# LayerNorm of x + residual on one core: another order and another cut of the 27 DMA transfers

## The chip, the core and the metric

The kernel runs on one core of a Trainium2 chip. The core has a tensor engine (PE), a vector engine (VectorE, DVE in the profile), a scalar engine (ScalarE, ACT), GpSimd (POOL) and a sync engine (SyncE, SP) that here only issues DMA transfers. Sixteen DMA engines move data between HBM (the large outer memory) and SBUF (the on-chip memory of 128 partitions). The metric is the device time of one execution in microseconds.

## The reference

```python
def setup_inputs():
    batch, seq, dim = 16, 1024, 512
    ...

def reference(x, residual, gamma, beta, eps):
    z = x + residual
    mean = np.mean(z, axis=-1, keepdims=True)
    var = np.var(z, axis=-1, keepdims=True)
    z_norm = (z - mean) / np.sqrt(var + eps)
    return (gamma * z_norm + beta).astype(np.float32)
```

x, residual and the output have 16 x 1024 = 16,384 vectors of 512 numbers in float32, 33.55 MB each. Each vector is normalised by itself.

## The kernel before

**Rows.** The 16,384 vectors are spread over 128 partitions, 128 to each. The kernel counts in "rows": row j is the j-th vector of every partition, 128 x 512 numbers or 256 KB, and there are 128 rows. They form two blocks of 64; within a block, the 64 vectors of a partition lie one behind the other in HBM (line 76), so a transfer of n rows reads or writes one run of n x 2 KB for each partition.

**Buffers.** SBUF holds `zbuf` with 64 rows, into which x is loaded and from which the output is stored, and `rbuf` with 32 rows, into which the residual is loaded. Row j uses place j mod 64 of the one and j mod 32 of the other. Both are rings: a load of a later row may start only when the row that had its place is done with it.

**Compute.** Work goes in turns of 4 rows, 32 turns in all, the same for every plan. For each turn, in order:
- POOL adds x and residual into `rbuf` (line 178), after the loads that hold these rows have landed.
- ACT takes the negative mean of each row (line 201), the sum of squares around it (line 211) and the standard deviation of the 4 rows (line 220).
- DVE computes (z + negative mean) x gamma into `zbuf` (line 239), the reciprocal `rstd` (line 247), and then times `rstd` plus beta (line 253). The semaphore `rstd` says that the turn's rows of `rbuf` are free, the semaphore `out` that its output is ready.

PE is used only at the start, to spread gamma and beta over the partitions (line 131).

**Transfers.** All loads and stores are issued by SP, in the order of the string PLAN (line 19). A word is a kind (x, r for residual, o for output), the first row and the number of rows: `x4+12` loads rows 4 to 15 of x. Each transfer has its own semaphore. Before it issues a transfer, SP waits for what that transfer needs, and all later transfers wait behind it (lines 145 to 160):

```python
if kind == "x":
    while gone < len(stores) and stores[gone][0] < lo + n - Z_ROWS:
        nc.sync.wait_ge(so[gone], 16)
        ...
elif kind == "r":
    if lo + n > R_ROWS:
        last = (lo + n - R_ROWS) // TURN - 1
        nc.sync.wait_ge(s_rstd[last % Z_TURNS], last // Z_TURNS + 1)
    ...
else:
    if lo + n > seen:
        nc.sync.wait_ge(s_out, lo + n)
```

So an x load waits until the stores that read its places of `zbuf` have landed; a residual load waits until DVE is done with the rows 32 earlier; a store waits for the output of its last row. After the last issue, SP waits for all stores (lines 163 to 167). The plan of before has 27 transfers: 10 of x, 10 of the residual and 7 of the output. The first two are issued ahead of the others, at the start of the program (lines 269 to 277).

Of the kernel before, what the change touches and what calls it, by code (L numbers as in the profile page):

```python
# [15 lines left out]
R_ROWS = 32  # L16


PLAN = """
x0+4 r0+4 x4+12 r4+16 x16+12 r20+12 x28+12 x40+16 x56+8  # L20
r32+16 o0+24 r48+16 x64+24 r64+16 o24+24 r80+16 x88+16
r96+12 o48+16 x104+8 r108+8 x112+16 r116+12
o64+24 o88+16 o104+16 o120+8
"""


ADDS = [4] * 32
# [11 lines left out]
def kernel(  # L39
# [22 lines left out]
    moves = []  # L62
    for word in PLAN.split():
        kind, (lo, n) = word[0], map(int, word[1:].split("+"))
# [248 lines left out]
```

## Time and profile before

| what | value |
|---|---|
| median of 5 runs | 237.93 us (237.88 to 238.36) |
| the profiled execution | 237.91 us |
| its span, from the first to the last instruction | 236.6 us |
| data moved | 100.67 MB: 67.11 MB read, 33.55 MB written |
| mean rate over the span | 426 GB/s |
| first store issued | at 63.55 us, after x loads up to row 63 and residual loads up to row 47 |
| last load landed | near 197.8 us |
| last store issued | at 225.4 us |

Times within the profile are microseconds from the start of the span. "Busy" is the time in which an engine executes instructions; for the DMA it is the share of time in which its 16 engines move packets. In a table of instructions, a row gives the start, the busy time, the engine, the line, the operation with its output and inputs, how many are merged in the row, and in brackets how long the engine had been idle before and what released it. In a table of waits, a row gives who waited for whom, the time in total, the number of waits and the longest. In a table of windows, the columns are the window, its length, the busy time and count of each engine, the tensor engine's clock, the DMA share and GB/s; packets are counted whole, so a short window can show more than 1. Issuing a DMA takes SP about 0.33 us and is not the transfer itself.

### The profile page before, as it was taken

The page shows a single profiled execution, that of the slowest core. Times are in us where ns is not written, and L with a number is a line of the kernel's source. Part 1 is how long each engine was busy: PE and PEld are TensorE (multiplying, and loading weights), DVE is VectorE, ACT ScalarE, POOL GpSimd, SP SyncE. Part 2 cuts the span into 40 slices and gives each one's busy share as a digit, 9 for nine tenths or more (in the row PEclk, how much of TensorE's full clock was granted, in tenths as well). Part 3 has the DMA queues.
Part 4 walks back from the last instruction along what each step waited for, and adds up shares of the span by engine and source line. Part 5 has one row for each costly group of instructions (what it writes and reads, how often), then busy time and mean ns, then how long its engine had stood idle before and what let it go on. Part 6 is the DMA issues. An engine that isn't in the chain of part 4 may idle for free.

```text
span 236.6 us, 988 instructions
## 1 busy us (share of the span) xinstructions
PE 3.7 (2%) x4; PEld 1.2 (0%) x4; DVE 177.3 (75%) x290; ACT 184.0 (78%) x545; POOL 144.1 (61%) x36
## 2 busy tenths in 40 slices
PE   0600000000000000000000000000000000000000
PEld 0100000000000000000000000000000000000000
DVE  0009009999996299979997999899999999879900
ACT  2090099999972999799979998899999999799100
POOL 0600899994009990999179926899939275970000
DMA  8999999999999999999999999999999999999997
GB/s 301 454 454 392 461 407 457 443 443 391 429 465 399 440 446 471 416 399 416 427 474 457 393 432 421 421 427 432 413 435 460 414 432 461 416 421 443 432 410 316
DMA packets 3892, 100.67 MB, mean 426 GB/s; under 512 B 434, under 2 KB 434, under 8 KB 436
## 3 DMA queue, kind: packets, MB, share of 16 engines
q1 hardware_dynamic: 3888, 100.67, 99.3%
q10 hardware_dynamic: 4, 0.00, 0.0%
HBM read 67.11 MB, written 33.55 MB: 426 GB/s over the span
## 4 chain that ended last, share of the span: by engine, by line
ACT 44%; DMA 37%; POOL 8%; DVE 6%; issue 1%; SPq 0%; DVEq 0%; POOLq 0%
DMA rbuf<-in_residual_dram 37%; ACT junk_s L211 22%; ACT junk_m L201 19%; POOL rbuf L178 8%; DVE zbuf L239 5%; ACT std L220 2%; DVE zbuf L253 1%; DVE rstd L247 0%; SPq L140 0%; DVEq L231 0%; POOLq L175 0%
## 5 line engine op out<-in xcount | busy, mean ns | idle before, releaser
L178 POOL TENSOR_TENSOR rbuf<-zbuf,rbuf 128x2048 f32<-128x2048 f32 x32 | 143.9, 4522 | 67.0 <-DMA rbuf<-in_residual_dram 57.1
L239 DVE SCALAR_TENSOR_TENSOR zbuf<-rbuf,nm,gamma_p 128x512 f32<-128x512 f32 x128 | 87.1, 743 | 44.9 <-ACT std L220 44.9
L201 ACT ACTIVATE junk_m<-rbuf 128x512 f32<-128x512 f32 x128 | 74.3, 580 | 30.9 <-POOL rbuf L178 30.8
L211 ACT ACTIVATE junk_s<-rbuf,nm 128x512 f32<-128x512 f32 x128 | 88.8, 694 | 1.0
L253 DVE SCALAR_TENSOR_TENSOR zbuf<-zbuf,rstd,beta_p 128x512 f32<-128x512 f32 x128 | 87.1, 744 | 1.1
L211 ACT ACTIVATION_READ_ACCUMULATOR junk_s<-rbuf,nm 128x1 f32 x128 | 23.9, 187 | 0.0
L201 ACT ACTIVATION_READ_ACCUMULATOR junk_m<-rbuf 128x1 f32 x128 | 23.9, 187 | 0.0
L220 ACT ACTIVATE std<-ssq,eps_t 128x4 f32<-128x4 f32 x32 | 9.5, 297 | 1.0
L247 DVE RECIPROCAL rstd<-std 128x4 f32<-128x4 f32 x32 | 5.5, 171 | 0.0
L192 ACT ACT_TABLE_LOAD x1 | 1.3, 1283 | 2.7 <-PEq L60 2.7
L131 PE MATMUL gamma_p<-gb_row,ones 1*128 1x512 f32 x2 | 2.0, 1120 | 6.8 <-DMA gb_row<-in_gamma_dram 6.8
L131 PE MATMUL beta_p<-gb_row,ones 1*128 1x512 f32 x2 | 1.9, 1056 | 0.0
L126 DVE MEMSET ones<- 1x128 f32 x1 | 0.2, 165 | 2.0 <-PEq L60 2.0
L131 PEld LDWEIGHTS beta_p<-gb_row,ones 1*128 1x128 f32 x2 | 0.7, 332 | 1.0 <-DMA gb_row<-in_beta_dram 0.5
L131 PEld LDWEIGHTS gamma_p<-gb_row,ones 1*128 1x128 f32 x2 | 0.5, 304 | 6.8 <-issue 6.8
L294 POOL MEMSET const-float32-0.0<- 128x1 f32 x1 | 0.1, 99 | 0.2 <-issue 0.2
L294 POOL MEMSET const-bfloat16-1.0<- 128x1 bf16 x1 | 0.1, 102 | 0.0
L294 POOL MEMSET const-uint8-127<- 128x1 uint8 x1 | 0.1, 102 | 0.0
L294 POOL MEMSET const-float32-1.0<- 128x1 f32 x1 | 0.1, 99 | 0.0
L127 DVE MEMSET eps_t<- 128x1 f32 x1 | 0.1, 59 | 0.0
## 6 DMA issues: line engine op xcount, KB each, us to landing
rbuf<-in_residual_dram SPq DMA_DIRECT2D x5, 4096.0 KB, 21.5
out_dram<-zbuf SPq DMA_DIRECT2D x3, 6144.0 KB, 30.1
zbuf<-in_x_dram SPq DMA_DIRECT2D x3, 4096.0 KB, 19.3
out_dram<-zbuf SPq DMA_DIRECT2D x3, 4096.0 KB, 26.1
zbuf<-in_x_dram SPq DMA_DIRECT2D x3, 3072.0 KB, 28.9
rbuf<-in_residual_dram SPq DMA_DIRECT2D x3, 3072.0 KB, 23.4
zbuf<-in_x_dram SPq DMA_DIRECT2D x1, 6144.0 KB, 23.9
zbuf<-in_x_dram SPq DMA_DIRECT2D x2, 2048.0 KB, 43.2
```

The costliest lines, as they stand in the source:

```text
L126: nc.vector.memset(ones[:, :], 1.0).then_inc(s_const, 1)
L127: nc.vector.memset(eps_t[:, :], float(eps)).then_inc(s_const, 1)
L131: nc.tensor.matmul(dest[:, :], ones[:, :], gb_row[:, k * D : (k + 1) * D], start=True, stop=True).then_inc(s_pe, 1)
L178: nc.gpsimd.tensor_tensor(out=z, in0=part(zbuf, Z_ROWS, lo, n), in1=z, op=ALU.add).then_inc(s_sum[lo // TURN % R_TURNS], 1)
L192: act.preload_act_table_set("sqrt_and_others")
L201: i = act.activation(out=junk_m[k][:, :], in_=part(rbuf, R_ROWS, r, 1), func=ACT.Identity, scale=-inv_d, accum_out=column(nm, r),)
L211: i = act.activation(out=junk_s[k][:, :], in_=part(rbuf, R_ROWS, r, 1), func=ACT.Square, bias=column(nm, r), accum_out=column(ssq, r),)
L220: act.activation(out=column(std, rows[0], TURN), in_=column(ssq, rows[0], TURN), func=ACT.Sqrt, bias=eps_t[:, 0:1], scale=inv_d,).then_inc ...
L239: dve.scalar_tensor_tensor(out=part(zbuf, Z_ROWS, r, 1), in0=part(rbuf, R_ROWS, r, 1), scalar=column(nm, r), in1=gamma_p[:, :], op0=ALU.ad ...
L247: dve.reciprocal(out=column(rstd, rows[0], TURN), in_=column(std, rows[0], TURN)).then_inc(s_rstd[j], 1)
L253: i = dve.scalar_tensor_tensor(out=z, in0=z, scalar=column(rstd, r), in1=beta_p[:, :], op0=ALU.mult, op1=ALU.add,)
L294: nc = _bacc.Bacc("TRN2", target_bir_lowering=False, num_devices=1)
```

## The change

Only the string PLAN changes. The compute instructions and their order stay as they are; the order, the sizes and with them the waits of SP's transfers change.

```diff
-PLAN = """
-x0+4 r0+4 x4+12 r4+16 x16+12 r20+12 x28+12 x40+16 x56+8
-r32+16 o0+24 r48+16 x64+24 r64+16 o24+24 r80+16 x88+16
-r96+12 o48+16 x104+8 r108+8 x112+16 r116+12
-o64+24 o88+16 o104+16 o120+8
-"""
+PLAN = """x0+4 r0+4 x4+12 r4+16 r20+12 x16+12 r32+4 x28+12 o0+8 x40+24 r36+16 o8+16 r52+12 x64+24 r64+16 o24+24 r80+16 x88+4 r96+8 x92+20 o48+16 r104+12 x112+16 r116+12 o64+24 o88+24 o112+12 o124+4"""
```

- The first four transfers stay. r20 and x16 trade places.
- Four rows of the residual (r32+4) are loaded ahead of x28, and the first store, now of 8 rows, follows x28. Before it stood behind the loads of x40, x56 and r32+16 too.
- x40+16 and x56+8 become one transfer of 24 rows; r32+16 and r48+16 become r32+4, r36+16 and r52+12; the first 24 rows of output are stored as 8 and 16 in place of 24.
- x88+16 and x104+8 become x88+4 and x92+20; r96+12 and r108+8 become r96+8 and r104+12.
- The last 64 rows are stored as 24, 24, 12 and 4 in place of 24, 16, 16 and 8.

There are now 28 transfers: 9 of x, 11 of the residual and 8 of the output. All lines below the plan move up by 5.

## The prediction

> **What bounds the kernel now.** I read the page's first table, then its DMA line, then the Sync queue's waits, then the start times of GpSimd's adds, which date the landings. The busiest engines leave much of the span free, and the 16 DMA engines leave almost none:
>
> ```profile
> PE 3.7 (2%) x4; PEld 1.2 (0%) x4; DVE 177.3 (75%) x290; ACT 184.0 (78%) x545; POOL 144.1 (61%) x36
> ...
> DMA  8999999999999999999999999999999999999997
> ...
> q1 hardware_dynamic: 3888, 100.67, 99.3%
> ```
>
> ScalarE (ACT) is busy 184.0 of 236.6 us. The one DMA queue that carries the data is busy 99.3% of all 16 engines' span, and the only slices below 9 tenths are the first and the last. The chain of waits names ACT for 44% and a residual load for 37%, but that chain follows single releases; the transfers behind it queue without a hole. The queue's own waits say the same from the issuing side:
>
> ```profile
> SPq L140 <- DVE rstd L247: 113.3, 7, 44.0
> SPq L140 <- DVE zbuf L253: 65.7, 5, 24.6
> SPq L140 <- DMA out_dram<-zbuf: 34.7, 3, 13.3
> ```
>
> SyncE (SP) waits 213.7 us (113.3 + 65.7 + 34.7), yet the DMA engines stay busy: each wait is spent while earlier transfers still run. So the time is: start, plus the sum of all transfers one after another, plus the last landing. An order changes it only if it leaves the DMA engines without work, or changes the cost of the transfers themselves.
>
> **The price of a transfer.** An add starts about 0.06 us after the load that it waited for, so these rows date landings:
>
> ```profile
> 24.57 31.39 POOL L178 TENSOR_TENSOR rbuf<-zbuf,rbuf 128x2048 f32<-128x2048 f32 x7 [12.38 <-DMA rbuf<-in_residual_dram]
> 70.88 17.94 POOL L178 TENSOR_TENSOR rbuf<-zbuf,rbuf 128x2048 f32<-128x2048 f32 x4 [14.92 <-DMA rbuf<-in_residual_dram]
> 95.17 17.99 POOL L178 TENSOR_TENSOR rbuf<-zbuf,rbuf 128x2048 f32<-128x2048 f32 x4 [6.35 <-DMA rbuf<-in_residual_dram]
> 119.60 17.98 POOL L178 TENSOR_TENSOR rbuf<-zbuf,rbuf 128x2048 f32<-128x2048 f32 x4 [6.44 <-DMA rbuf<-in_residual_dram]
> 143.88 9.01 POOL L178 TENSOR_TENSOR rbuf<-zbuf,rbuf 128x2048 f32<-128x2048 f32 x2 [6.29 <-DMA rbuf<-in_residual_dram]
> 153.59 17.99 POOL L178 TENSOR_TENSOR rbuf<-zbuf,rbuf 128x2048 f32<-128x2048 f32 x4 [0.70 <-DMA zbuf<-in_x_dram]
> 175.62 4.53 POOL L178 TENSOR_TENSOR rbuf<-zbuf,rbuf 128x2048 f32<-128x2048 f32 x1 [4.03 <-DMA zbuf<-in_x_dram]
> 180.52 4.53 POOL L178 TENSOR_TENSOR rbuf<-zbuf,rbuf 128x2048 f32<-128x2048 f32 x1 [0.37 <-DMA rbuf<-in_residual_dram]
> 190.23 4.53 POOL L178 TENSOR_TENSOR rbuf<-zbuf,rbuf 128x2048 f32<-128x2048 f32 x1 [5.17 <-DMA zbuf<-in_x_dram]
> 197.82 4.53 POOL L178 TENSOR_TENSOR rbuf<-zbuf,rbuf 128x2048 f32<-128x2048 f32 x1 [3.05 <-DMA rbuf<-in_residual_dram]
> ```
>
> Two pairs of neighbours hold one load each: x88+16 takes 153.59 - 143.88 = 9.71 us and r108+8 takes 180.52 - 175.62 = 4.90 us. So a row of the plan costs (9.71 - 4.90) / 8 = 0.601 us and a transfer 4.90 - 8 x 0.601 = 0.09 us beside its rows. The other gaps, less this price, show what a **turn from loads to stores** costs. 24.57 to 70.88 holds 76 rows in 6 transfers (46.22 by the price, +0.09), and the next 24.29 us o0+24 and r48+16 (24.22, +0.07): 0.16 for the first turn. 95.17 to 119.60 (40 rows, 24.43, +0.21) and the stretch to 143.88 (24.28, +0.06): 0.27 for the second. 153.59 to 175.62 holds r96+12, o48+16 and x104+8 (21.91, measured 22.03): 0.12. r116+12, ahead of the last stores, took 7.59 where 7.30 was due: 0.29. From 197.82 to the last landing near 236.5 come 64 rows in four stores (38.82 by the price, 38.7 measured), so 0.1 of that comes back. A turn costs 0.12 to 0.29, 0.2 in the middle; turns from stores to loads show nothing of their own.
>
> **The change, part by part.**
> *Bytes.* Both plans move 128 rows of x, residual and out: nothing.
> *One transfer more* (28 for 27): +0.09 us. The upper end is the other small transfer shown: r0+4 was issued at 0.44 and landed 7.1 later, at 7.54; x0+4 landed at 4.9; 2.64 for 4 rows is 0.24 over 4 x 0.601, with the start of the kernel in it.
> *One turn more.* Before, stores follow loads four times (o0, o24, o48, o64); after, five times (o0+8, o8+16, o24, o48, o64): +0.12 to +0.29, I take 0.18.
> *One more issue on SP* (0.33 us) and one more wait at its end lie beside running transfers; without that cover they would cost 0.35.
> *Swap of x16 and r20:* the rows that need either (16 to 27) need both; the adds of rows 4 to 15 run on meanwhile. Nothing.
> *The last store of 4 rows* in place of 8 shortens nothing: it waits in the queue, not for compute. Before, the last store was issued at 225.4 and landed 11.2 us later, of which its own 8 rows are 4.9, so 6.3 us of other stores ran ahead of it.
>
> **Where a wait could empty the queue.** The cover of a wait is the work still queued when the waiting instruction issues. A first byte takes about 1.0 us from the issue (the first issue is at 0.00, no DMA is busy before 1.00). Compute goes by its rows: an add 4.5 us, ACT 5.77 a turn of 4 rows, DVE 2.85 to rstd and 2.75 more to the output.
> - o0+8 waits for the output of row 7. ACT ends that turn near 35.0, DVE near 40.5; r32+4 and x28+12 hold the queue until 24.4 + 40 rows in 4 transfers = 48.8. Cover 8.3.
> - x64+24 waits for o8+16 to land, with only r52+12 queued: 7.3, where the shortest such cover before was 9.7 (x88+16 behind r80+16). x112+16 behind r104+12 is alike: 7.3.
> - r64+16 waits for rstd of row 47: r36+16 lands near 78.1 (24.4, 88 rows, 7 transfers, a turn), the add ends at 82.7, ACT ends rows 36 to 47 at 100.0, rstd 102.8. The queue runs until r36's 78.1 + 17.2 (o8+16, r52+12, a turn) + 14.5 (x64+24) = 109.8. Cover 7.0.
> - r96+8 (rstd of row 71, near 137.5) has r80 and x88+4 ahead of it until 146.4: 8.9. Behind it stand x92+20 and o48+16, which need nothing later.
> - o112+12 waits for row 123: the last load lands near 198.0, outputs of rows 120 to 123 are ready near 219.8, and o64+24 and o88+24 run to 227.1: 7.3. o124+4, ready near 225.5, has 8.9.
> All exceed the 1.0 by 6 us or more, so no hole is due, and nothing of the moved waits reaches the end.
>
> **Sum.** +0.09 + 0.18 = +0.27 us on the profiled execution (237.91 us, a span of 236.6 and 1.3 around it); the median of the runs is 237.93. Forecast **238.2 us**, +0.1%.
>
> **A rule that speaks against it.** Measured, a transfer of 4 rows (1024 KB) takes 2.64 us in the queue at most, and an extra transfer 0.09 to 0.24. The Trainium skill, "DMA: Bandwidth & Descriptors", section "Anatomy of one DMA", gives each DMA a fixed cost of about 2.0 us, on the GpSimd path; were that serial here, the 28th transfer alone would make 239.9. The rows above contradict that for queued transfers: landings follow at 0.601 us a row with 0.09 between.
>
> **Rivals.**
> 1. *Nothing at all* (0.2): turn and transfer vanish in the engines' own spread: 237.9. For it: the last turn gave back 0.1 of 0.29.
> 2. *The turns cost more* (0.15). Two turns now stand where all engines run in step; in the trace's packet records the turn from r32+16 to o0+24 has the largest single delay, 0.60 us on one 32 KB packet. With 0.24 for the transfer and 0.4 for the turn: 238.55, slower.
> 3. *The queue runs dry* at x64+24 (0.04), and x112+16 alike, since 12 rows are all that is behind the store waited for. It decides once landing, wait and first byte take over 7.3 us. Each us beyond costs a us at each of the two: 1 us short gives 240.2. Against it: 1.0 us measured, and the same shape with 9.7 left no hole.
> 4. *The engines end together* (0.06). At the end a few engines run alone:
>
> ```profile
> 234.50:235.00 0.50, 0.00 (x0) 0.00 (x0) 0.00 (x0) 0.00 (x0) 0.00 (x0) 1.00 0.84 360
> 235.00:235.50 0.50, 0.00 (x0) 0.00 (x0) 0.00 (x0) 0.00 (x0) 0.00 (x0) 1.00 0.16 66
> 235.50:236.00 0.50, 0.00 (x0) 0.00 (x0) 0.00 (x0) 0.00 (x0) 0.00 (x0) 1.00 0.08 33
> ```
>
> The DMA share (second column from the end) falls to 0.16 and 0.08: after 235.00 that adds up to 0.12 us of all engines ((0.16 + 0.08) x 0.5), and the last landing comes 1.5 us later. If the new order evened out two thirds of it (an estimate), 1.0 us would go: 237.2. Against it: each engine still gets the same bytes, and one turn more adds spread.
>
> **How the numbers follow.** Forecast 0.55 (238.0 to 238.4), rival 1 0.2, rival 2 0.15, rival 3 0.04, rival 4 0.06. The range 237.7 to 238.65 holds the forecast, rivals 1 and 2, and leaves out about a tenth and the outer parts of these. A measurement of this kernel tells about 0.2% (0.48 us) from no change: faster is rival 4 (0.06), slower rivals 2 and 3 (0.19), within 0.2% the rest (0.75).
>
> **What would show it.** Right: the queue again at 99% of its span, no slice but the first and last below 9; the add released by r36+16 near 78, that by r52+12 near 95, the last one near 198.1; o124+4 issued near 225.5 and landing near 236.8. Wrong: a slice in the middle below 9, an add late by a microsecond or more against these times, the last store landing soon after its issue, or a row price other than 0.60.

## The result

The changed kernel takes 238.68 us (median of 21 runs, 237.93 to 240.12), the kernel before 237.92 us (41 runs, 237.63 to 238.63): a ratio of 1.0036, 95% interval 1.0025 to 1.0046, or +0.86 us by the ratio. It is slower, by three times the 0.27 us that were forecast.

The profiled execution took 238.31 us with a span of 237.0, 0.4 us more than before. The page still shows a kernel that waits for its transfers:

```profile
PE 3.7 (2%) x4; PEld 1.2 (0%) x4; DVE 177.2 (75%) x290; ACT 183.9 (78%) x545; POOL 144.0 (61%) x36
...
DMA  8999999999999999999999999999999999999997
...
q1 hardware_dynamic: 4032, 100.67, 99.3%
```

The engines' busy times are within 0.1 us of before, the DMA engines are at 99.3% again, and no slice in the middle falls below 9. So no wait emptied the queue. The rows of the adds date the landings (start and busy time in us, engine, line, operation, how many; in brackets the idle time before and what ended it):

```profile
24.44 13.43 POOL L173 TENSOR_TENSOR rbuf<-zbuf,rbuf 128x2048 f32<-128x2048 f32 x3 [12.35 <-DMA rbuf<-in_residual_dram]
38.98 22.47 POOL L173 TENSOR_TENSOR rbuf<-zbuf,rbuf 128x2048 f32<-128x2048 f32 x5 [1.10 <-DMA zbuf<-in_x_dram]
78.56 31.40 POOL L173 TENSOR_TENSOR rbuf<-zbuf,rbuf 128x2048 f32<-128x2048 f32 x7 [17.11 <-DMA rbuf<-in_residual_dram]
119.97 17.98 POOL L173 TENSOR_TENSOR rbuf<-zbuf,rbuf 128x2048 f32<-128x2048 f32 x4 [10.02 <-DMA rbuf<-in_residual_dram]
144.20 13.50 POOL L173 TENSOR_TENSOR rbuf<-zbuf,rbuf 128x2048 f32<-128x2048 f32 x3 [6.24 <-DMA rbuf<-in_residual_dram]
163.71 13.50 POOL L173 TENSOR_TENSOR rbuf<-zbuf,rbuf 128x2048 f32<-128x2048 f32 x3 [6.01 <-DMA zbuf<-in_x_dram]
...
197.82 13.51 POOL L173 TENSOR_TENSOR rbuf<-zbuf,rbuf 128x2048 f32<-128x2048 f32 x3 [2.78 <-DMA rbuf<-in_residual_dram]
```

With the prediction's price (0.601 us a row, 0.09 a transfer) the stretches between these rows show where time is lost. From 24.44 to 78.56 come 88 rows in 7 transfers, 53.52 by the price and 54.12 measured: 0.60 lost. This stretch holds the turn from x28+12 to o0+8 and ends with r36+16, the load ahead of the next turn, so the rows alone don't say at which of the two. The trace also has a record of when each of the 16 engines landed its share of a transfer. By the last share, x28+12 took 0.57 longer than its price and r36+16 0.01: the first turn cost it. From 78.56 to 119.97 (o8+16 to the landing of r64+16) come 68 rows in 4 transfers: 41.23 due, 41.41 measured, 0.18 lost. The next two stretches, with the turns at o24+24 and at o48+16 (the latter seen from 163.71 on), cost 0.01 and about 0.1.

One sum is the same for both plans. Between the landings of r4+16 and r64+16 lie 156 rows in either plan, in 10 transfers before and 11 after. This stretch took 119.60 - 24.57 = 95.03 us before and 119.97 - 24.44 = 95.53 after: +0.50, of which 0.09 is the transfer. The rest of the kernel is as long as before: from the add of r64+16 to the last landing it is 236.5 - 119.60 = 116.9 us before and 236.9 - 119.97 = 116.9 after. (The span grows by 0.4 and not by 0.5, since r4+16 landed 0.13 earlier in this execution.)

### The profile page after: what moved, and what is told of

Its sections match the earlier page's. It is cut to its first block, busy times and chain, and to the rows that moved or that the text cites. A ratio compares the mean times of both kernels' runs of the same rounds, so it can differ in the third digit from the quotient of the medians.

```text
span 237.0 us, 990 instructions
## 1 busy us (share of the span) xinstructions
PE 3.7 (2%) x4; PEld 1.2 (0%) x4; DVE 177.2 (75%) x290; ACT 183.9 (78%) x545; POOL 144.0 (61%) x36
## 3 DMA queue, kind: packets, MB, share of 16 engines
q1 hardware_dynamic: 4032, 100.67, 99.3%
## 4 chain that ended last, share of the span: by engine, by line
ACT 43%; DMA 36%; POOL 8%; DVE 6%; issue 1%; SPq 0%; ACTq 0%; DVEq 0%; POOLq 0%
DMA rbuf<-in_residual_dram 26%; ACT junk_s L206 22%; ACT junk_m L196 19%; DMA zbuf<-in_x_dram 10%; POOL rbuf L173 8%; DVE zbuf L234 5%; ACT std L215 2%; DVE zbuf L248 1%; SPq L135 0%; DVE rstd L242 0%; ACTq L189 0%; DVEq L226 0%; ACTq L194 0%; POOLq L170 0%; ACTq L190 0%
```

## The experiments

Theory E: the early extra turn from loads to stores costs the time. Its rivals, as they came up: N, every turn costs alike; S, a short store behind a load makes the turn dear; C, a thin queue ahead of a wait costs time even where it doesn't run empty; D, another order of the loads costs it; Q, the name of C at first; and that the middle or the end of the new plan costs it. In the expectations of the first four runs E is called A, N is called B, and the last rival is called C; in the later ones C is the thin queue. All times are against the kernel before on the same chip, with the 95% interval of the ratio.

### Which half of the plan

`after_again` is the changed kernel once more.

> The changed plan once more, as the yardstick for the runs beside it. Theory A (the first turn from loads to stores, x28 to o0+8, is dear and varies from run to run): +0.3 to +1.0 us against the kernel before, single times spread over 2 us, and in the profile x28+12 landing 0.5 us or more later than its 12 rows cost. Theory B (every turn and every transfer costs a little, 0.1 to 0.3 us): +0.2 to +0.4 with a spread like that of before.

Measured: 1.0021 (1.0005 to 1.0037), median 238.21 beside 237.89, single times 237.86 to 239.83.

`start_only` has the changed plan up to r80+16 and the plan of before behind it:

```diff
-... r80+16 x88+4 r96+8 x92+20 o48+16 r104+12 x112+16 r116+12 o64+24 o88+24 o112+12 o124+4
+... r80+16 x88+16 r96+12 o48+16 x104+8 r108+8 x112+16 r116+12 o64+24 o88+16 o104+16 o120+8
```

> The changed plan up to r80+16, the plan of before from x88+16 on: 28 transfers, 5 turns. Theory A: as slow as the whole change, +0.3 to +1.0, with the same spread of single times. Theory B: +0.2 to +0.4, tight. Theory C (the new end, stores of 24, 24, 12 and 4 rows, and the new middle cost the time): within 0.1 us of before.

Measured: 1.0029 (1.0015 to 1.0043), single times 238.03 to 239.82. `rest_only` is the other half: the plan of before up to r80+16, the changed one behind it.

> The plan of before up to r80+16, the changed plan from x88+4 on: 27 transfers, 4 turns. Theories A and B: within 0.15 us of before. Theory C: +0.4 or more, since the whole cost sits in this half.

Measured: 0.9995 (0.9986 to 1.0003), single times 237.61 to 238.19. The whole cost, with the spread of single times, sits in the first part of the plan. The new middle and the new end, the last store of 4 rows included, cost nothing that can be measured, and gain nothing.

### Is it turns as such, or something at this one

`late_turn` adds a turn to the plan of before at another place:

```diff
-... r64+16 o24+24 r80+16 x88+16 ...
+... r64+16 o24+16 r80+16 o40+8 x88+16 ...
```

> The plan of before with o24+24 cut into o24+16 and, after r80+16, o40+8: 28 transfers and 5 turns as in the change, but the extra turn comes near 139 us, when the engines are 0.5 us or more out of step. Theory A: within 0.2 us of before. Theory B: +0.2 to +0.4, as much as the change.

Measured: 1.0076 (1.0055 to 1.0098), median 240.25. Neither theory had that: it is over twice the price of the change. Two things were tried for it, a short store and a thin queue. `split_store` keeps the four turns, and puts a store of 8 rows at the first:

```diff
-... r32+16 o0+24 r48+16 ...
+... r32+16 o0+8 o8+16 r48+16 ...
```

> The plan of before with its first store cut in two, o0+8 and o8+16 one behind the other: 28 transfers, 4 turns, and the first turn at the same place, but into a store of 8 rows (16 KB packets). Theory S (what makes a turn dear is a short store behind the load): +0.3 to +1.0 us, the load r32+16 ending 0.5 us or more late. Theory N (what makes it dear is one more turn, wherever it stands): +0.1, the price of a transfer.

Measured: 1.0003 (0.9995 to 1.0012). Theory S falls: a store of 8 rows behind a load costs no more than one of 24, and a 28th transfer without a turn costs 0.07 us by the ratio, in keeping with 0.09. `first12` starts from start_only and cuts the early stores 12 and 12:

```diff
-... x28+12 o0+8 x40+24 r36+16 o8+16 r52+12 ...
+... x28+12 o0+12 x40+24 r36+16 o12+12 r52+12 ...
```

> The early first store of the change with 12 and 12 rows in place of 8 and 16, and the plan of before from x88+16 on: 28 transfers, 5 turns. Theory S: clearly less than start_only, +0.1 to +0.3. Theory N: the same as start_only, +0.5 or more.

Measured: 1.0095 (1.0067 to 1.0122), median 240.22: far more than start_only, against S and N alike. Row 11's output is ready late: o0+12 issues at 46.21, and x28+12 has landed by 48.7, so 2.5 us were queued. `two_short_late` and `late_turn_16` separate the store's size from the queue:

```diff
two_short_late
-... r80+16 x88+16 r96+12 o48+16 x104+8 ...
+... r80+16 o48+8 x88+16 r96+12 o56+8 x104+8 ...
late_turn_16
-... o24+24 r80+16 x88+16 r96+12 o48+16 x104+8 ...
+... o24+16 r80+16 o40+16 x88+16 r96+12 o56+8 x104+8 ...
```

> The plan of before with o48+16 cut into o48+8 behind r80+16 and o56+8 behind r96+12: 28 transfers, 5 turns, two of them into stores of 8 rows, with a full queue behind each. Theory S: +0.8 to +2, both loads ending late. Theory N: +0.3 to +0.7. Theory Q (the slowness of late_turn came from its short queue of 3 us ahead of r80+16, not from the turn): within 0.3.

Measured: 1.0011 (0.9999 to 1.0023), median 238.04 beside 237.96.

> Like late_turn, with o24+16 ahead of r80+16 and the same short queue there, but o40+16 behind it and o56+8 behind r96+12: 28 transfers, 5 turns. Theory S: r80+16 ends on time, r96+12 is the late one. Theory Q: r80+16 ends late again, by 0.5 us or more in the mean of the engines. Theory N: +0.3 to +0.7, and neither place stands out.

Measured: 1.0093 (1.0080 to 1.0107), median 240.00. A turn with a full queue is cheap, and the kernel whose r80+16 issues with 3 to 4 us queued pays 2 us, with a store of 16 rows as with one of 8. That is what theory Q, later C, expects. `four_short_late` counts what a late turn costs:

```diff
-... r80+16 x88+16 r96+12 o48+16 x104+8 ...
+... r80+16 o48+4 x88+8 o52+4 x96+8 o56+4 r96+12 o60+4 x104+8 ...
```

> The plan of before with o48+16 cut into four stores of 4 rows, each behind a load, all with 10 us or more queued: 31 transfers, 7 turns. Theory N with the prices of the prediction: 4 x 0.09 + 3 x 0.18 = +0.9. If a turn that stands late and with a full queue costs next to nothing: +0.3 to +0.5, the transfers alone.

Measured: 1.0022 (1.0014 to 1.0031), +0.5 us by the ratio and +0.36 by the medians. Four transfers at 0.09 are 0.36, so three further turns there cost about 0.05 each by these numbers, and 0.13 at the upper end of the interval. Theory N falls: a turn has no fixed price.

### The queue by itself

`thin_cover` has the thin queue of late_turn and no added turn:

```diff
-... o24+24 r80+16 x88+16 r96+12 o48+16 x104+8 ...
+... o24+16 r80+16 x88+16 r96+12 o40+8 o48+16 x104+8 ...
```

> The plan of before with o24+24 cut into o24+16 and an o40+8 that joins o48+16 behind r96+12: 28 transfers, 4 turns, so no turn is added, but r80+16 is issued with only 3 us queued and x88+16 is issued when that store has landed, as in late_turn. Theory C: +1.5 to +2.5, as late_turn. Theory E and theory N (turns alone cost): +0.1.

Measured: 1.0067 (1.0053 to 1.0081), median 239.64. The thin queue costs 1.6 us by the ratio, without any added turn. Its adds, dated as above:

```profile
119.84 17.98 POOL L178 TENSOR_TENSOR rbuf<-zbuf,rbuf 128x2048 f32<-128x2048 f32 x4 [6.32 <-DMA rbuf<-in_residual_dram]
139.73 9.02 POOL L178 TENSOR_TENSOR rbuf<-zbuf,rbuf 128x2048 f32<-128x2048 f32 x2 [1.92 <-DMA rbuf<-in_residual_dram]
149.42 17.99 POOL L178 TENSOR_TENSOR rbuf<-zbuf,rbuf 128x2048 f32<-128x2048 f32 x4 [0.68 <-DMA zbuf<-in_x_dram]
177.42 4.53 POOL L178 TENSOR_TENSOR rbuf<-zbuf,rbuf 128x2048 f32<-128x2048 f32 x1 [10.01 <-DMA zbuf<-in_x_dram]
```

119.84 to 139.73 holds o24+16 and r80+16: 19.41 due, 19.89 measured, 0.48 lost. x88+16 then takes 9.69, nothing lost. 149.42 to 177.42 holds r96+12, o40+8, o48+16 and x104+8: 26.80 due, 28.00 measured, 1.20 lost. The issues of SP tell how much was queued:

```profile
126.05 0.33 SPq L140 DMA_DIRECT2D rbuf<-in_residual_dram  x1
129.54 0.33 SPq L140 DMA_DIRECT2D zbuf<-in_x_dram  x1
144.61 0.33 SPq L140 DMA_DIRECT2D rbuf<-in_residual_dram  x1
```

The second row is x88+16, which waits for o24+16 to land. So r80+16, issued at 126.05, had 129.5 - 126.05 = 3.5 us ahead of it, and r96+12, issued at 144.61, had the rest of x88+16, which lands at 149.4: 4.7 us. Both are more than the 1.0 us from an issue to the first byte, and the DMA engines hardly go idle (from 126 to 130 us the DMA share is 1.06, packets counted whole; by the packet records one of the 16 is without a packet for some 0.7 us in all near 155 us, and none before). By the landing records, the 16 engines end o24+16 within 0.54 us of each other, r80+16 within 1.37 and r96+12 within 2.11: some engines fall behind and stay behind to the end. One packet of r80+16 takes 2.27 us where 1.21 is usual, one of r96+12 2.25 where 0.92 is usual. `cover6` has the same form with more queued:

```diff
-... o24+16 r80+16 x88+16 r96+12 o40+8 o48+16 x104+8 ...
+... o24+20 r80+16 x88+16 r96+12 o44+4 o48+16 x104+8 ...
```

> As thin_cover, with o24+20 and o44+4 in place of o24+16 and o40+8: 28 transfers, 4 turns, r80+16 issued with 5.7 us queued and r96+12 with 6.7, where before they had 8.1 and 9.1. Theory C (a thin queue costs by degrees): +0.4 to +1.0, so that the 6.8 us of the changed plan would explain its cost. Theory E (the early turn costs; a queue of 6 us is enough): within 0.15 of before.

Measured: 1.0001 (0.9992 to 1.0010), median 237.94 beside 237.85. The same two rows of the adds, and SP's issues of r80+16 and x88+16:

```profile
119.73 17.98 POOL L178 TENSOR_TENSOR rbuf<-zbuf,rbuf 128x2048 f32<-128x2048 f32 x4 [6.32 <-DMA rbuf<-in_residual_dram]
141.56 9.04 POOL L178 TENSOR_TENSOR rbuf<-zbuf,rbuf 128x2048 f32<-128x2048 f32 x2 [3.84 <-DMA rbuf<-in_residual_dram]
```

```profile
125.96 0.33 SPq L140 DMA_DIRECT2D rbuf<-in_residual_dram  x1
132.10 0.33 SPq L140 DMA_DIRECT2D zbuf<-in_x_dram  x1
```

21.83 us for 36 rows in 2 transfers, 21.82 due, with 132.1 - 125.96 = 6.1 us queued. So a queue of 6.1 us is enough and one of 3.5 isn't. In the changed plan one of the thinnest queues is that at r64+16. These are the issues of r64+16, o24+24, r80+16 and x88+4:

```profile
103.31 0.33 SPq L135 DMA_DIRECT2D rbuf<-in_residual_dram  x1
106.07 0.34 SPq L135 DMA_DIRECT2D out_dram<-zbuf  x1
126.29 0.33 SPq L135 DMA_DIRECT2D rbuf<-in_residual_dram  x1
134.58 0.33 SPq L135 DMA_DIRECT2D zbuf<-in_x_dram  x1
```

r64+16 is issued at 103.31; it landed at 119.91 and needs 9.7 of that for itself, so 6.9 us were queued (7.0 was forecast). r80+16 is issued at 126.29, and o24+24 ahead of it landed when x88+4 was issued, at 134.58: 8.3 us. At x64+24 (issued at 88.65, r52+12 ahead of it landed at 95.6) it was 7.0, at x112+16 (173.61, r104+12 landed at 180.7) 7.1, at o112+12 (220.25, o88+24 landed at 227.1) 6.9. All are above the 6.1 that cost nothing. So a thin queue accounts for late_turn and late_turn_16, and not for the change. In first12 it can have cost the 1.3 us that are lost up to the landing of x40+24. Another 1.2 are lost at r36+16, ahead of o12+12, with 16.9 us queued when it was issued (at 54.95; x40+24 landed at 71.81), and these it doesn't explain.

### The early turn by itself

`one_first_store` takes the early turn out of the changed plan and leaves all the rest:

```diff
-... x28+12 o0+8 x40+24 r36+16 o8+16 r52+12 ...
+... x28+12 x40+24 r36+16 o0+24 r52+12 ...
```

> The changed plan with its two first stores joined again to o0+24 behind r36+16, all the rest as changed: 27 transfers, 4 turns. Theory E (the early extra turn, x28 to o0+8, costs the time): within 0.15 us of before. Theory C (thin covers cost the time: a wait that leaves only some 7 us or less of queued transfers): also about 0, since joining them lets r36+16 land 5 us earlier and thickens the cover ahead of r64+16 from 6.8 to 11 us. Theory D (the order of loads, r32+4 ahead of x28, or x40+24 as one): +0.3 or more stays.

Measured: 0.9992 (0.9982 to 1.0002), median 237.85 beside 237.90, single times 237.64 to 238.08. The cost is gone, and the spread too; theory D falls. On this chip the early turn ran beside it in early_thick (below), not in the changed plan itself. The profiled execution of one_first_store took 238.08 us, the longest of its runs; its adds:

```profile
24.42 13.43 POOL L178 TENSOR_TENSOR rbuf<-zbuf,rbuf 128x2048 f32<-128x2048 f32 x3 [12.52 <-DMA rbuf<-in_residual_dram]
...
73.87 17.96 POOL L178 TENSOR_TENSOR rbuf<-zbuf,rbuf 128x2048 f32<-128x2048 f32 x4 [12.43 <-DMA rbuf<-in_residual_dram]
95.74 13.49 POOL L178 TENSOR_TENSOR rbuf<-zbuf,rbuf 128x2048 f32<-128x2048 f32 x3 [3.91 <-DMA rbuf<-in_residual_dram]
120.05 17.96 POOL L178 TENSOR_TENSOR rbuf<-zbuf,rbuf 128x2048 f32<-128x2048 f32 x4 [10.82 <-DMA rbuf<-in_residual_dram]
```

From 24.42 to 95.74 come 116 rows in 8 transfers, 70.44 due and 71.32 measured: the single first turn, r36+16 to o0+24, cost 0.88 in this execution, all of it by the landing of r36+16. From 95.74 to 120.05 it is 24.31 against 24.22. `early_thick` starts from start_only; it keeps the early turn and thickens the queue behind it:

```diff
-... x16+12 r32+4 x28+12 o0+8 x40+24 r36+16 o8+16 r52+12 ...
+... x16+12 x28+12 r32+8 o0+8 x40+24 r40+12 o8+16 r52+12 ...
```

> An early first store as in the change, but with r32+8 ahead of it and r40+12 behind x40+24, so that rows 36 to 39 are worked on earlier and r64+16 and r80+16 are issued with 12 and 13 us queued, where the change leaves 6.8 and 7.9: 28 transfers, 5 turns, the plan of before from x88+16 on. Theory E: +0.3 to +0.8, as start_only. Theory C: within 0.2.

Measured: 1.0015 (1.0003 to 1.0027), between the two theories. start_only, early_thick and the changed plan were run again on one chip, beside cover6.

> start_only once more, beside early_thick_2 on one chip. Theories C and E: +0.3 to +0.8 again.

Measured: 1.0020 (1.0010 to 1.0031).

> early_thick once more, beside start_only_2 on one chip. Theory E: no more than 0.15 us below start_only_2. Theory C: within 0.15 of before and at least 0.3 below start_only_2.

Measured: 1.0028 (1.0017 to 1.0038). With thick queues the early turn costs as much as without; with cover6 beside it, theory C falls for the change.

> The changed plan a third time. +0.3 to +0.8 with single times up to 240. If this profile falls on a slow one: the DMA engines land their shares of one transfer 2 us or more apart from some turn on, as in late_turn, first12 and thin_cover, and the place where that begins is the place that costs. Theory E: at x28 to o0+8 or at r36 to o8+16. Theory C: near 103 to 127 us, where r64+16 and r80+16 are issued.

Measured: 1.0040 (1.0023 to 1.0057), median 238.62, single times 238.15 to 239.82; its profiled execution took 238.58. Two more profiled executions of the changed plan:

> The changed plan once more, one profile only. If it is a long execution (239 us or more), its loss shows at one turn as engines that land 2 us or more apart. Theory E: x28+12 to o0+8 or r36+16 to o8+16, before 90 us. If the loss sits at a later turn (r64+16, x92+20 or r116+12), the early turn is not what makes the long executions.

> The same look again; the same expectations as for after_look4.

Measured: 238.22 and 238.71, so no profile fell on one of 239 or more. The second is next to the median of the changed kernel, and its adds show where it loses:

```profile
24.46 13.43 POOL L173 TENSOR_TENSOR rbuf<-zbuf,rbuf 128x2048 f32<-128x2048 f32 x3 [12.52 <-DMA rbuf<-in_residual_dram]
...
78.84 31.39 POOL L173 TENSOR_TENSOR rbuf<-zbuf,rbuf 128x2048 f32<-128x2048 f32 x7 [17.37 <-DMA rbuf<-in_residual_dram]
120.36 17.98 POOL L173 TENSOR_TENSOR rbuf<-zbuf,rbuf 128x2048 f32<-128x2048 f32 x4 [10.13 <-DMA rbuf<-in_residual_dram]
144.62 13.50 POOL L173 TENSOR_TENSOR rbuf<-zbuf,rbuf 128x2048 f32<-128x2048 f32 x3 [6.27 <-DMA rbuf<-in_residual_dram]
...
190.88 4.52 POOL L173 TENSOR_TENSOR rbuf<-zbuf,rbuf 128x2048 f32<-128x2048 f32 x1 [0.69 <-DMA zbuf<-in_x_dram]
198.68 13.50 POOL L173 TENSOR_TENSOR rbuf<-zbuf,rbuf 128x2048 f32<-128x2048 f32 x3 [3.28 <-DMA rbuf<-in_residual_dram]
```

78.84 - 24.46 = 54.38 against 53.52: 0.86 lost. By the landing records the last share of x28+12 came 0.63 late and that of r36+16 another 0.30, so both of the first two turns took part. 120.36 - 78.84 = 41.52 against 41.23: 0.29, of which 0.19 came at r64+16, the load ahead of o24+24. 0.04 is lost in the next stretch. And r116+12, the load ahead of the last stores, took 198.68 - 190.88 = 7.80 where 7.30 was due: 0.50 near 198 us. The profile of after_third, at 238.58 the second longest, loses 0.49 there too; in the other three it is 0.00 to 0.07. That is the sign that the expectation set against the early turn as the origin of the long executions, though neither of the two is as long as 239 us. The plan of before lost 0.29 there in its own profile.

### The first stretch in all profiles

The stretch from r4+16 to r64+16, 156 rows in each of these plans:

| plan up to r64+16 | turns, transfers | us from add to add, one profile each |
|---|---|---|
| as before (before, rest_only, two_short_late, four_short_late, cover6, thin_cover, late_turn, late_turn_16) | 1, 10 | 95.03, 95.30, 95.16, 95.32, 95.22, 95.26, 95.45, 95.41: mean 95.27 |
| first store cut, no turn added (split_store) | 1, 11 | 95.37 |
| stores joined (one_first_store) | 1, 10 | 95.63 |
| early turn (changed plan five times, start_only twice, early_thick twice) | 2, 11 | 95.53, 95.68, 95.61, 95.54, 95.90, 95.68, 95.75, 95.83, 95.59: mean 95.68 |

The early turn with its transfer costs 0.41 us there in the mean, and the first and the last group don't overlap. The profile of before, 95.03, is the lowest of its group. One row doesn't fit: one_first_store is as long as the early turns in this stretch, though its median equals that of before; its profile fell on its longest run, and others of it were not seen.

The landing records of the same profiles part the turns. How much later than its price the load ahead of a store lands (us, last share):

| plan up to r64+16 | ahead of the first store | ahead of the second turn |
|---|---|---|
| as before, split_store (9 profiles) | r32+16: 0.16 to 0.62, mean 0.45 | r64+16: 0.00 to 0.42, mean 0.07 |
| one_first_store (1) | r36+16: 0.88 | r64+16: 0.00 |
| early turn (9) | x28+12 or r32+8: 0.55 to 0.94, mean 0.72 | r36+16 or r40+12: 0.00 to 0.30, mean 0.12 |

So in the mean the first turn of the kernel is the dear one of the two, in every kind of plan. With the early store it is 0.27 dearer, and the turn that comes behind it, the added one, costs 0.12.

## Why the prediction was wrong

**Right: what bounds the kernel.** Order matters only through holes and through the price of transfers. The DMA share and the compute engines' busy times didn't change, and the landings came where the sum put them: r36+16's add at 78.56 (near 78 was forecast), the last at 197.82 (198.1), o124+4 landing near 236.9 (236.8). The add that r52+12 was to release near 95 can't be seen, since the adds run on without a gap from 78.56; the landing record has r52+12 at 95.6.

**Right: the covers.** No wait in the changed plan emptied the queue, cover6 shows that 6 us are enough, and r64+16 had 6.9. But the reason given for them was too weak. The prediction let a wait cost nothing as long as more than 1.0 us was queued; thin_cover lost 1.6 us with 3.5 and 4.7 queued and the engines hardly idle. Had the plan come down to such a queue, the forecast would have missed it.

**Right: the transfer, the swap, the end.** The 28th transfer costs about 0.09 (split_store 1.0003, four_short_late). The Trainium skill, "DMA: Bandwidth & Descriptors", section "Anatomy of one DMA", gives each DMA on the GpSimd path a fixed cost of about 2.0 us. Here SP issues the transfers, and four_short_late adds four of them, and three turns, for 0.36 to 0.5 us in all: in this queue no such cost is added to the time. The swap of x16 and r20, the joined loads, the middle and the last store of 4 rows cost nothing (one_first_store, rest_only).

**Wrong: the step "One turn more ... +0.12 to +0.29, I take 0.18".** The early turn with its transfer measures 0.41 in the profiles, 0.32 for the turn alone, and its kernels are 0.24 to 0.95 us slower by their medians and ratios. Two things were mis-sized. First, the price came from a single profile, that with the lowest first stretch of eight (95.03 against a mean of 95.27); its first turn showed 0.16, where the same turn shows 0.26 to 0.69 in the other profiles of that plan (24.5 to the add of r48+16, less 70.44). Second, the turns were taken as one population with a middle, so that moving the first of them forward was put at nothing, and they aren't: three added late turns cost about 0.05 each (four_short_late), the added second turn 0.12 in the mean, and the first turn 0.72 in the early plans against 0.45 in the plan of before. So most of what the profiles show came from the first turn, which both plans have, and not from there being one more.

**The case that came.** It is rival 2, "the turns cost more", with 0.24 for the transfer and 0.4 for the turn, 238.55. Its total was near, though the transfer was cheap and the turn took it all. Its reason, that single packets are delayed at a turn, is what the packet records show at x28+12 (below); of its two turns only the first was dear. It had a chance of 0.15; the highest of the four readings, from one execution, was 0.29. The range ended 0.03 below the median.

**Open.** The turn's 0.32 and the transfer are about half of the 0.76 to 0.86 us by which the changed kernel is slower. Its profiles took 237.92 to 238.71 us. Of its 43 timed runs 13 took 239 us or more, up to 240.12; of the 153 runs of before none took more than 238.86. No profile shows such a run, so where these lose their further 0.5 to 1.5 us isn't known. The two longest profiles lose 0.5 at the last turn, at r116+12. That one_first_store has no such run among 11 fits the early turn as their origin but doesn't show it: start_only_2, with the early turn, has none among 12 either, and two_short_late, without it, has one of 239.30. Why the first turn is dearer than later ones, and dearer still in the early plans, also stays open. The size of the store (split_store) and the thin queue (cover6, early_thick_2) are excluded; the order of the loads around it and the time at which it comes are not, and no run moves the first store forward without adding a turn.

## What to carry to other kernels

When the transfers fill the whole time, the order of loads and stores still has a price: the turn from loads to stores, which here cost from nothing to 0.9 us and was dearest at the first store of the kernel. Take it from several profiles of the same kernel, since one may fall on the cheap end, and give a cost that varies that much a range to match. Keep transfers queued ahead of every wait of the issuing engine: 6.1 us were enough here, 3.5 and 4.7 in one plan were not, and what lies between was not measured. "The queue doesn't run empty" isn't enough.

## What was not expected of the hardware

- A load issued with 3.5 us of transfers still queued cost 1.6 us in all (thin_cover, with a second wait at 4.7), with no more than one DMA engine in 16 without a packet, for some 0.7 us; with 6.1 us queued the same form cost nothing (cover6, 1.0001).
- At a turn from loads to stores it is the last packets of the load that take longer. In the packet records of the changed kernel, 30 of the 128 packets of x28+12 (24 KB, 0.91 to 0.92 us each otherwise) take up to 0.496 us more than 0.912. They start between 46.1 and 47.6 us, the first packet of o0+8 at 48.4, and the packets of that store take 0.611 us, within 0.04. In one_first_store, where a load follows x28+12, no packet of it takes more than 0.925.
- The 16 engines can drift apart and stay so to the end: in late_turn their shares of r80+16 land 2.53 us apart and those of the last store 3.18, and the kernel ends with the last of them.
